# Rotations of k and q in PSUM, and low parts of plain weights in two operations

## The chip, the cores and the metric

The kernel runs on one core of one Trainium2 chip. The metric is the device time of one execution in microseconds (us), the median of several runs. TensorE (PE) multiplies, VectorE (DVE), ScalarE (ACT) and GpSimd (POOL) do the elementwise work, SyncE (SP) issues the transfers. SBUF is the on-chip memory, PSUM the eight banks that TensorE writes its products to.

## The reference

A two-layer streaming encoder step, in fp32: 1024 frames of a new stream (the prompt) and 64 frames of a running one (the sample), 1088 columns of 1024 features. Layer 0 is a gated short convolution. Layer 1 is latent attention with rotated parts of q and k, and this is where most of the change lies:

```
def apply_rope(x, cos, sin):
    x1, x2 = xf[..., :QK_ROPE_DIM // 2], xf[..., QK_ROPE_DIM // 2:]
    out = jnp.concatenate([x1 * cos - x2 * sin, x2 * cos + x1 * sin], axis=-1)

def mla_project(h, pos, w_in, q_norm_g, w_qb, kv_norm_g):
    p = h @ w_in                       # q_lat 256, kv_lat 128, k_rope 32, z 1024
    q = (rms_norm(q_lat, q_norm_g) @ w_qb).reshape(B, T, N_HEADS, QK_DIM)
    q_rope = apply_rope(q[..., QK_NOPE_DIM:], cos[:, None, :], sin[:, None, :])
    k_rope = apply_rope(k_rope, cos, sin)
    c_kv = rms_norm(kv_lat, kv_norm_g)
    return q, c_kv, k_rope, z
```

After it come attention (16 heads, a mask by chunks of 64 frames for the prompt, 512 cached keys for the sample), `silu(z) * o` times an output matrix, a residual add and a last norm.

## The kernel before

**Accuracy.** Every fp32 product is three products of a reduced type: each operand is split into a high part (a copy by ScalarE into that type, `hi`) and a low part (`raw - hi`), and hi·hi, hi·lo and lo·hi are added up in PSUM. So each weight of 128x1024 costs a transfer (L287), a copy by ScalarE (L288) and a subtraction. `load_w` (L274) gives the subtraction to GpSimd (L292) unless it is told otherwise. The conv weights that are used in combinations are split by other lines (L636, L637), which stay as they are.

**Stages.** Columns are taken in three chunks of 384, 384 and 320 (`CHK`), features in eight tiles of 128. Layer 0 fills the time to about 510 us. Then comes the front of layer 1 (to about 590 us), sample attention (to 675), prompt attention, and from about 985 us the output projection.

**The front of layer 1.** Nine tiles of latents are made with `latent_mm` and leave PSUM by `latent_evac` (VectorE, L1059). The q latents are normed into `QNH`, `QNL` (high and low) with `QNS` for the sample (L1011). Then the loop at L1141 makes k's 32 rotated rows for each chunk c: 16 products with `wrs`, ScalarE copies half the result to SBUF (`t1`, L1155), and VectorE adds the other half (L1156), multiplies by the norm `r1` (L1157), swaps the halves of the 32 rows (`stream_shuffle`, L1158), multiplies by sin (L1159) and cos (L1160) and adds (L1161). In the trace `t1` and `t2` are called kt. In between, the generator `c_norm` norms the kv latents: it makes `csh` and `csl` (L351, L352) of each chunk, which TensorE sums over the partitions with a matrix of ones, and `sample_q` makes the sample's q from `QNS`.

Then `q_rope(g, c)` (L1204) rotates q for four groups of heads, g, and three chunks, c, twelve times: six products into a bank of PSUM, shuffle (L1212), times sin on GpSimd (L1213), times cos on VectorE (L1216), sum (L1217), high part by ScalarE (L1219), low part on VectorE (L1222), and two transfers out (L1224). `t1` and `t2` are called qt in the trace, `qlo` is qrl.

**What sets the order.** Between these steps stand half tiles of the gate projection (`z_stream`, L1014: 24 products for each chunk, then one multiplication on VectorE out of PSUM, L1031, and the next weight after a tile's first chunk). How many half tiles follow each step is written in tables (`ZA`, `ZC`, `ZR`, L973). Within that, a scheduler at build time orders each engine's queue. All matmuls of these stages are recorded at one line, L301. PSUM is one tile PS of eight banks; `split_psum` divides it into rings, here z of banks 0 and 1 and g of banks 2 to 7, and `gps` takes the next bank of a ring in turn, so a product waits until the last reader of that bank is done.

Of the kernel before, what the change touches and what calls it, by code (L numbers as in the profile page):

```python
# [11 lines left out]
F32 = mybir.dt.float32  # L12
# [29 lines left out]
def r32(ap):  # L42
    return ap.bitcast(F32)
# [166 lines left out]
def kernel(ctx, tc, xT, small, w1, w2, w3, w3r, wpair, wqr, wv, wkT, w4,  # L210
# [3 lines left out]
    V, A, G, PE, SP = nc.vector, nc.scalar, nc.gpsimd, nc.tensor, nc.sync  # L214
# [9 lines left out]
    def nm(s):  # L224
        cnt[0] += 1
        return f"{s}_{cnt[0]}"

    PS = ctx.enter_context(tc.tile_pool(name="ps", bufs=1, space=PSUM)).tile([P, 8, 512], F32, name="PS")
    turns = {}

    def split_psum(**first):

        turns.clear()
        turns.update({k: [v, 0] for k, v in first.items()})

    def gps(tag="g", size=1):
        (b0, b1), k = turns[tag]
        turns[tag][1] = (k + size) % (b1 - b0)
        return PS[:, b0 + k:b0 + k + size, :].rearrange("p b n -> p (b n)")
# [27 lines left out]
    def ordered(ins):  # L267
        if keep_order[0]:
            tc.keep_in_program_order(ins)

    WN = [1024, 2]
    hi_on, lo_on = [None], [None]

    def load_w(src, n, view=None, into=None, lo_engine=None, cuts=None, shared=False):  # L274
        raw = wp[0].tile([P, WN[0]], F32, tag="wraw", name=nm("wraw"), bufs=3)
        if into is None:
            hi = wp[0].tile([P, WN[0]], F32R, tag="whi", name=nm("whi"), bufs=WN[1])
            lo = wp[0].tile([P, WN[0]], F32R, tag="wlo", name=nm("wlo"), bufs=WN[1])
        else:
            hi, lo = into  # L280
        if cuts:
            def part(a, b):
                ordered(A.copy(out=hi[:, a:b], in_=raw[:, a:b]))
                ordered((lo_engine or G).tensor_sub(lo[:, a:b], raw[:, a:b], r32(hi[:, a:b])))
            return hi, lo, lambda a, b: SP.dma_start(out=raw[:, a:b], in_=src[:, a:b]), part
        dst = raw[:, :n] if view is None else view(raw[:, :n])
        SP.dma_start(out=dst, in_=src)  # L287
        ins = A.copy(out=hi[:, :n], in_=raw[:, :n])  # L288
        hi_on[0] = ins.ins
        ordered(ins)  # L290
        m = n // 2 if shared else n
        ins = (lo_engine or G).tensor_sub(lo[:, :m], raw[:, :m], r32(hi[:, :m]))  # L292
        lo_on[0] = ins.ins
        ordered(ins)
        if shared:
            V.tensor_sub(lo[:, m:n], raw[:, m:n], r32(hi[:, m:n]))
        return hi, lo
# [86 lines left out]
    def xh(k, c0, c1):  # L384
        return XHV[:, k, c0:c1]
# [153 lines left out]
    def new_u(ct, sc):  # L539
        u = p1.tile([P, SC + 4], F32, tag="u", name=nm("u"), bufs=1)  # L540
        if sc == 0:
            V.memset(u[:, 0:2], 0.0)
        return u

    def new_z():
        return p1.tile([P, SC], F32, tag="z", name=nm("z"), bufs=1)
# [251 lines left out]
    for ct in range(STD):  # L798
        if ct == 0:
            u, z = new_u(ct, 0), new_z()  # L800
# [68 lines left out]
        else:  # L869
            for pi, part in enumerate(PARTS):  # L870
# [4 lines left out]
                for c in range(2):  # L875
                    ps = conv_mm(c, W, (KD, 0)[c])
                    if ct == 1 and pi == c == 0:
                        rest()
                    if pi == c == 0:
                        u, z = new_u(ct, 0), new_z()  # L880
# [55 lines left out]
    for dt in range(KD):  # L936
        wh, wl = load_w(w2[dt], 1024)
        g = sm[:, C_NG + 8 + dt:C_NG + 9 + dt]
# [3 lines left out]
        for c, (c0, c1) in enumerate(CHK):  # L942
            n = c1 - c0
            x = xr[c]
            ps = gps()
# [23 lines left out]
    p1.release()  # L969


    split_psum(z=(0, 2), g=(2, 8))
    ZA, ZC, ZR, ZQ, ZB, ZS = (0, 1), 1, (0, 2, 1, 1), (0, 1, 1, 1, 3, 0, 1, 0), (1, 2, 3), ((1, 2, 2, 1), (1, 2, 2, 1), (1, 2, 2, 1), (1, 2, 1, 0))  # L973
    SIL, ZG = ((0,), (1,), (2,), (3, 4), (5, 6)), (1, 1, 1, 0)
    pz = tc.alloc_tile_pool(name="pz", bufs=1, reuse_waits="tile")
# [17 lines left out]
    p3t = tc.alloc_tile_pool(name="p3t", bufs=1, reuse_waits="tile")  # L993

    cosb, sinb = SZ[:, 6, :], SZ[:, 7, :]
    ql = [SZ[:, 2, :], SZ[:, 3, :], SZ[:, 4, :]]
    kr = SZ[0:ROPE, 5, :]
# [3 lines left out]
    SHUF = [(i + 16) % 32 for i in range(32)]  # L1001
    r1 = acc1
# [5 lines left out]
    def split(hi, lo, src, lo_engine=None):  # L1008
        ins = A.copy(out=hi, in_=src)
        ordered(ins)  # L1010
        ordered((lo_engine or V).tensor_sub(lo, src, r32(hi)))  # L1011
        return ins.ins
# [82 lines left out]
    ps = latent_mm(2, 0)  # L1095
    q_rstd(1, sq1)
    latent_evac(2, 0, ps)
    ps = latent_mm(2, 1)
# [48 lines left out]
    for c, (c0, c1) in enumerate(CHK):  # L1147
        n = c1 - c0
        ps = gps("z")
        for k in range(KD):  # L1150
            mm(ps[:2 * ROPE, :n], wrs3[:, k, :], xh(k, c0, c1), k == 0, False)
            mm(ps[:2 * ROPE, :n], wrs3[:, k, :], xl(k, c0, c1), False, k == KD - 1)
        t1 = p3t.tile([P, 512], F32, tag="qt1", name=nm("kt1"), bufs=2)[:ROPE]
        t2 = p3t.tile([P, 512], F32, tag="qt2", name=nm("kt2"), bufs=2)[:ROPE]
        A.copy(out=t1[:, :n], in_=ps[ROPE:2 * ROPE, :n])  # L1155
        V.tensor_add(t1[:, :n], ps[:ROPE, :n], t1[:, :n])  # L1156
        V.tensor_mul(t1[:, :n], t1[:, :n], r1[:ROPE, c0:c1])  # L1157
        V.stream_shuffle(t2[:, :n], t1[:, :n], SHUF)  # L1158
        V.tensor_mul(t2[:, :n], t2[:, :n], sinb[:ROPE, c0:c1])  # L1159
        V.tensor_mul(t1[:, :n], t1[:, :n], cosb[:ROPE, c0:c1])  # L1160
        V.tensor_add(kr[:, c0:c1], t1[:, :n], t2[:, :n])  # L1161
        if c == 0:
            for f in range(2):
                split(QNH[:, f, :], QNL[:, f, :], ql[f], G if f else None)
    next(cns)
    SP.dma_start(out=o_kr, in_=kr)
    split(KR[0:32, :], KR[32:64, :], kr[:, :SEQ])

    def add_halves(out, ps3):

# [33 lines left out]
    def q_rope(g, c):  # L1204
        c0, c1 = CHK[c]
        n = c1 - c0
        wh, wl = (x[:, g * 256:(g + 1) * 256] for x in WR)
        ps = gps()
        gemm(ps[:, :n], lambda k: wh[:, k * P:(k + 1) * P], lambda k: wl[:, k * P:(k + 1) * P],
             lambda k: QNH[:, k, c0:c1], lambda k: QNL[:, k, c0:c1], 2)  # L1210
        t2 = p3t.tile([P, 512], F32, tag="qt2", name=nm("qt2"), bufs=2)
        ordered(V.stream_shuffle(t2[:, :n], ps[:, :n], SHUF))  # L1212
        G.tensor_mul(t2[:, :n], t2[:, :n], sinb[:, c0:c1])  # L1213
        yield
        t1 = p3t.tile([P, 512], F32, tag="qt1", name=nm("qt1"), bufs=2)
        ordered(V.tensor_mul(t1[:, :n], ps[:, :n], cosb[:, c0:c1]))  # L1216
        ordered(V.tensor_add(t1[:, :n], t1[:, :n], t2[:, :n]))  # L1217
        qh = p3t.tile([P, 512], F32R, tag="qrh", name=nm("qrh"), bufs=2)
        ordered(A.copy(out=qh[:, :n], in_=t1[:, :n]))  # L1219
        yield  # L1220
        qlo = p3t.tile([P, 512], F32R, tag="qrl", name=nm("qrl"), bufs=2)
        ordered(V.tensor_sub(qlo[:, :n], t1[:, :n], r32(qh[:, :n])))  # L1222
        for s, t in ((0, qh), (1, qlo)):
            SP.dma_start(out=qr_d[s, 4 * g:4 * g + 4, :, c0:c1].rearrange("h r t -> (h r) t"), in_=r32(t[:, :n]))  # L1224

# [39 lines left out]
    for g in range(4):  # L1265
# [3 lines left out]
        if g == 2:  # L1269
            ps = gps()  # L1270
# [142 lines left out]
    pk = tc.alloc_tile_pool(name="pk", bufs=1, reuse_waits="tile")  # L1413
# [285 lines left out]
    for n in ends:  # L1699
        if isinstance(n, int):  # L1700
            split_gated(448, 832, [n])
        else:
            name = n[0], H - 1, n[1]
# [122 lines left out]
    for dt in range(KD):  # L1826
# [136 lines left out]
```

## Time and profile before

| | |
|---|---|
| median of 3 runs | 1089.97 us (1088.22 to 1091.15) |
| the profiled execution | 1086.63 us, its span 1084.8 us, 1.83 us around it |
| mean granted clock of TensorE | 0.989 of full speed |
| PE busy | 1045.5 us (96%), 7123 matmuls |
| PE weight loads busy | 1002.3 us (92%) |
| DVE busy | 746.9 us (69%) |
| ACT busy | 638.2 us (59%) |
| POOL busy | 528.4 us (49%) |

Busy shares are means over stages that differ. A row of the timeline gives the start in us from the beginning of the span, the duration, the engine, the line, the operation, output <- inputs, shapes, how many, and in brackets the idle time ahead of it with what ended it. A row of the windows gives the stretch, its length, the busy us (and number of instructions) of PE, its weight loads, DVE, ACT and POOL, then TensorE's granted clock as a share of full speed, the DMA engines' busy share and GB/s.

### The profile page before, as it was taken

To read this page: it belongs to the slowest core of one execution; us is meant where nothing else is said; L and a number is where in the kernel's file an instruction comes from. 1 tells how busy PE (TensorE), PEld (TensorE's weight loads), DVE (VectorE), ACT (ScalarE), POOL (GpSimd) and SP (SyncE) were. 2 spreads that over 40 slices of the span, in tenths; PEclk is the share of its full clock that TensorE was granted. 3 is DMA by queue.
4 is the path that set the end of the run, shared out by engine and by line. 5 is a ranking of instruction groups with operands and counts; after the bars stand their busy time and mean duration, and the time that the engine had idled before them with its cause. 6 is when DMAs were issued, how large, how long until landed. Compare 5 with 4: busy or idle time off the path is not lost.

```text
span 1084.8 us, 19669 instructions
## 1 busy us (share of the span) xinstructions
PE 1045.5 (96%) x7123; PEld 1002.3 (92%) x7123; DVE 746.9 (69%) x1523; ACT 638.2 (59%) x1388; POOL 528.4 (49%) x446
## 2 busy tenths in 40 slices
PE   9979999999999999999898999999999999999997
PEld 8979999989999999999798999899999999898996
DVE  6787666756666545564997442688888888888346
ACT  6456676666666634344532434777877787786434
POOL 0476598896666622212443322354645555465225
PEclk9999999999999999999898999999999999999999
DMA  7244233333223244432232113544233412326225
GB/s 239 70 128 134 106 110 109 128 130 118 98 98 114 78 141 142 131 104 72 82 126 100 50 34 92 120 93 106 57 71 89 105 50 60 79 67 213 95 83 204
DMA packets 58145, 114.55 MB, mean 106 GB/s; under 512 B 8080, under 2 KB 32400, under 8 KB 58048
## 3 DMA queue, kind: packets, MB, share of 16 engines
q1 hardware_dynamic: 57840, 112.97, 34.3%
q8 instruction: 56, 0.92, 0.4%
q14 instruction: 41, 0.34, 0.1%
q10 hardware_dynamic: 144, 0.26, 0.1%
q0 software_dynamic: 64, 0.07, 0.0%
HBM read 79.27 MB, written 16.31 MB: 88 GB/s over the span
## 4 chain that ended last, share of the span: by engine, by line
PE 74%; DVE 11%; ACT 4%; POOL 3%; DMA 3%; issue 3%; SPq 1%; POOLq 0%; DVEq 0%; ACTq 0%
PE PS L301 52%; PE PS L1487 17%; PE PS L1526 5%; DMA QB<-stg 2%; DVE PS L488 1%; POOL wlo L292 1%; DVE OL L1011 1%; ACT PH L1539 1%; ACT stg L1603 1%; POOL R L565 1%; POOL R L513 0%; DMA wraw<-in_w 0%; DVE qt L1212 0%; DVE SZ L367 0%; SPq L1613 0%
## 5 line engine op out<-in xcount | busy, mean ns | idle before, releaser
L301 PE MATMUL PS<-R,whi 128*128 128x272 f32 (+2 forms) x1662 | 370.3, 312 | 14.8 <-ACT whi L288 4.4
L301 PEld LDWEIGHTS PS<-R,whi 128*128 128x128 f32 x1662 | 276.9, 191 | 18.9 <-ACT whi L288 5.1
L301 PE MATMUL PS<-R,wlo 128*128 128x272 f32 (+2 forms) x888 | 266.8, 312 | 2.3 <-POOL wlo L292 2.3
L292 POOL TENSOR_TENSOR wlo<-wraw,whi 128x1024 fp32r<-128x1024 f32 x36 | 88.6, 2462 | 185.5 <-ACT whi L288 172.8
L301 PEld LDWEIGHTS PS<-R,wlo 128*128 128x128 f32 x888 | 165.0, 191 | 3.4 <-POOL wlo L292 3.0
L1487 PE MATMUL PS<-KB,QB 96*128 96x512 f32 (+11 forms) x576 | 125.1, 354 | 1.1 <-DVE SZ L1031 0.6
L1521 POOL TENSOR_SCALAR Pt<-Pt,st 128x640 f32<-128x640 f32 (+3 forms) x64 | 61.4, 961 | 86.2 <-DVE st L1517 85.6
L1487 PEld LDWEIGHTS PS<-KB,QB 96*128 96x128 f32 (+1 forms) x576 | 94.3, 190 | 9.5 <-DVE PL L1543 1.1
L1504 DVE TENSOR_REDUCE st<-PS 128x1 f32<-128x1024 f32 (+7 forms) x128 | 94.7, 748 | 10.9 <-PE PS L1487 10.2
L1543 DVE TENSOR_TENSOR PL<-PS,PH 128x512 fp32r<-128x512 f32 (+3 forms) x192 | 98.7, 547 | 3.1 <-ACT PH L1539 1.8
L1539 ACT CAST PH<-PS 128x512 fp32r<-128x512 f32 (+3 forms) x192 | 85.3, 496 | 14.7 <-PE PS L1526 13.4
L1487 PE MATMUL PS<-PH,VB 128*128 128x256 f32 x320 | 76.5, 279 | 0.0
L637 POOL TENSOR_TENSOR wlo<-wraw,whi 128x1024 fp32r<-128x1024 f32 x26 | 62.5, 2404 | 26.8 <-ACT whi L636 26.5
L1487 PE MATMUL PS<-PL,VB 128*128 128x256 f32 x320 | 75.2, 281 | 0.2 <-DVE PL L1543 0.2
L1513 ACT ACTIVATE Pt<-PS,st 128x640 f32<-128x640 f32 (+3 forms) x64 | 62.1, 970 | 5.7 <-DVE st L1517 2.6
L301 PE MATMUL PS<-R,bhi 128*128 128x272 f32 x320 | 61.1, 289 | 2.3 <-DVE z L763 1.0
L1487 PEld LDWEIGHTS PS<-PH,VB 128*128 128x128 f32 x320 | 60.7, 190 | 1.3 <-DVE PL L1543 0.8
L1487 PEld LDWEIGHTS PS<-PL,VB 128*128 128x128 f32 x320 | 61.0, 191 | 0.7 <-DVE PL L1543 0.4
L288 ACT CAST whi<-wraw 128x1024 fp32r<-128x1024 f32 (+1 forms) x37 | 38.2, 1034 | 39.1 <-PE PS L301 20.6
L1526 PE MATMUL PS<-ident,Pt 128*128 128x128 f32 x416 | 55.4, 274 | 0.2 <-ACT Pt L1513 0.2
L1568 POOL TENSOR_TENSOR SZ<-SZ,ot 64x256 f32<-64x256 f32 x64 | 47.0, 744 | 11.6 <-DVE ot L1563 9.4
L301 PEld LDWEIGHTS PS<-R,bhi 128*128 128x128 f32 x320 | 49.6, 188 | 3.3 <-DVE z L763 1.2
(435 smaller groups left out, 2607.1 us busy)
## 6 DMA issues: line engine op xcount, KB each, us to landing
wraw<-in_w SPq DMA_DIRECT2D x83, 512.0 KB, 3.6
KB<-stg SPq DMA_DIRECT2D x32, 256.0 KB, 3.8
QB<-stg SPq DMA_DIRECT2D x32, 256.0 KB, 4.6
braw<-in_w SPq DMA_DIRECT2D x13, 512.0 KB, 4.4
QB<-qr_scratch SPq DMA_DIRECT2D x32, 128.0 KB, 3.0
x<-x_scratch SPq DMA_DIRECT2D x8, 416.0 KB, 3.2
xr<-in_xT SPq DMA_DIRECT2D x16, 192.0 KB, 2.5
x_scratch<-xr SPq DMA_DIRECT2D x16, 192.0 KB, 1.8
```

The costliest lines, as they stand in the source:

```text
L288: ins = A.copy(out=hi[:, :n], in_=raw[:, :n])
L292: ins = (lo_engine or G).tensor_sub(lo[:, :m], raw[:, :m], r32(hi[:, :m]))
L301: ins = PE.matmul(ps, lhsT, rhs, start=start, stop=stop, skip_group_check=more)
L637: ins = eng.tensor_sub(lo, src, r32(hi))
L1487: pin(PE.matmul(ps, lhsT, rhs, start=start, stop=stop))
L1504: pin(V.tensor_reduce(out=st[:, 0:1], in_=TL["S", h, i], axis=AX.XY, op=ALU.max, negate=True))
L1513: pin(A.activation(out=Pt, in_=TL.pop(("S", h, i)), func=AF.Exp, bias=st[:, 0:1], accum_out=st[:, 1:2]))
L1521: pin(G.tensor_scalar(Pt, Pt, st[:, 2:3], 1.0, op0=ALU.mult, op1=ALU.mult))
L1526: pin(PE.transpose(out=tp[:, j * P:(j + 1) * P], in_=TL["P", h, i][:, (j0 + j) * P:(j0 + j + 1) * P], identity=ident))
L1539: pin(A.copy(out=hi, in_=src))
L1543: pin(V.tensor_sub(lo, src, r32(hi)))
L1568: pin(G.tensor_mul(sz, sz, TL.pop(("ot", h, pr))[rows]))
```

## The change

Three edits.

1. `load_w`: where GpSimd forms the low part of a weight of 1024 columns, it does so in two subtractions of 512 columns.
2. PSUM is divided into z of banks 0 to 3 and g of banks 4 to 7 through the latents and the rotation of k; after that into z of 0 and 1 and g of 2 to 7 as before, the next bank of g being bank 4.
3. The rotations work in place in PSUM. For k: the sum, the product with `r1`, the shuffle, the product with cos and the last sum read PSUM, and the product with sin moves from VectorE to GpSimd. For q: product with cos, sum, high part and low part read PSUM, and the bank is held until the low part is made (L1222, before: L1216).

```
+        c = m // 2 if lo_engine is None and m == 1024 else m
+        for a in range(0, m, c):
+            ins = (lo_engine or G).tensor_sub(lo[:, a:a + c], raw[:, a:a + c], r32(hi[:, a:a + c]))
...
-    split_psum(z=(0, 2), g=(2, 8))
+    split_psum(z=(0, 4), g=(4, 8))
...
-        V.tensor_add(t1[:, :n], ps[:ROPE, :n], t1[:, :n])
-        V.tensor_mul(t1[:, :n], t1[:, :n], r1[:ROPE, c0:c1])
-        V.stream_shuffle(t2[:, :n], t1[:, :n], SHUF)
-        V.tensor_mul(t2[:, :n], t2[:, :n], sinb[:ROPE, c0:c1])
-        V.tensor_mul(t1[:, :n], t1[:, :n], cosb[:ROPE, c0:c1])
-        V.tensor_add(kr[:, c0:c1], t1[:, :n], t2[:, :n])
+        pk = ps[:ROPE, :n]
+        V.tensor_add(pk, pk, t1[:, :n])
+        V.tensor_mul(pk, pk, r1[:ROPE, c0:c1])
+        V.stream_shuffle(t2[:, :n], pk, SHUF)
+        G.tensor_mul(t2[:, :n], t2[:, :n], sinb[:ROPE, c0:c1])
+        V.tensor_mul(pk, pk, cosb[:ROPE, c0:c1])
+        V.tensor_add(kr[:, c0:c1], pk, t2[:, :n])
...
+    split_psum(z=(0, 2), g=(2, 8))
+    turns["g"][1] = 2
...
-        t1 = p3t.tile([P, 512], F32, tag="qt1", name=nm("qt1"), bufs=2)
-        ordered(V.tensor_mul(t1[:, :n], ps[:, :n], cosb[:, c0:c1]))
-        ordered(V.tensor_add(t1[:, :n], t1[:, :n], t2[:, :n]))
+        t1 = ps[:, :n]
+        ordered(V.tensor_mul(t1, t1, cosb[:, c0:c1]))
+        ordered(V.tensor_add(t1, t1, t2[:, :n]))
...
-        ordered(A.copy(out=qh[:, :n], in_=t1[:, :n]))
+        ordered(A.copy(out=qh[:, :n], in_=t1))
...
-        ordered(V.tensor_sub(qlo[:, :n], t1[:, :n], r32(qh[:, :n])))
+        ordered(V.tensor_sub(qlo[:, :n], t1, r32(qh[:, :n])))
```

Three places in which the queues differ. Lines of the changed kernel lie a few further down: L1156 to L1158 are L1159 to L1161, L1160 and L1161 are L1163 and L1164, L292 is L294, L352 is L354, and the product with sin is L1162.

First VectorE, in the rotation of k, from the second chunk's first sum (kt_612 and kt_613 before, kt_612 and kt_613_6000 after) to `csl`. Before:

```order
L1156 TENSOR_TENSOR kt_612_5977<-PS,kt_612_5977 32x384
L1161 TENSOR_TENSOR SZ<-kt_610_5948,kt_611_5949 32x384
L1157 TENSOR_TENSOR kt_612_5977<-kt_612_5977,acc_100 32x384
L1158 STREAM_SHUFFLE kt_613_5978<-kt_612_5977 32x384
L1156 TENSOR_TENSOR kt_614_6002<-PS,kt_614_6002 32x320
L1159 TENSOR_TENSOR kt_613_5978<-kt_613_5978,SZ 32x384
L1160 TENSOR_TENSOR kt_612_5977<-kt_612_5977,SZ 32x384
L1157 TENSOR_TENSOR kt_614_6002<-kt_614_6002,acc_100 32x320
L1161 TENSOR_TENSOR SZ<-kt_612_5977,kt_613_5978 32x384
L1158 STREAM_SHUFFLE kt_615_6003<-kt_614_6002 32x320
L352 SCALAR_TENSOR_TENSOR csl_6049<-SZ,eps_88,csh_6048 128x384
```

And after:

```order
L1159 TENSOR_TENSOR PS<-PS,kt_612_5999 32x384
L1164 TENSOR_TENSOR SZ<-PS,kt_611_5971 32x384
L1160 TENSOR_TENSOR PS<-PS,acc_100 32x384
L1161 STREAM_SHUFFLE kt_613_6000<-PS 32x384
L1163 TENSOR_TENSOR PS<-PS,SZ 32x384
L1159 TENSOR_TENSOR PS<-PS,kt_614_6024 32x320
L1164 TENSOR_TENSOR SZ<-PS,kt_613_6000 32x384
L1160 TENSOR_TENSOR PS<-PS,acc_100 32x320
L354 SCALAR_TENSOR_TENSOR csl_6071<-SZ,eps_88,csh_6070 128x384
```

The product with sin is gone from this queue, every other operation has PS in place of one SBUF input, `csl` moves ahead of the third chunk's shuffle, and the last sum of a chunk (SZ<-PS) stands behind the next chunk's first sum, as before.

Second GpSimd at the same place. Before:

```order
L292 TENSOR_TENSOR CKL<-wraw_5925,CKH 128x1024
L292 TENSOR_TENSOR wlo_5915<-wraw_5913,whi_5914 128x1024
L1011 TENSOR_TENSOR QNL<-SZ,QNH 128x1088
L1192 TENSOR_TENSOR wk_6260<-wraw_6258,wk_6259 128x256
L292 TENSOR_TENSOR wlo_6113<-wraw_6111,whi_6112 128x1024
```

And after:

```order
L294 TENSOR_TENSOR CKL<-wraw_5946,CKH 128x512 x2
L294 TENSOR_TENSOR wlo_5935<-wraw_5933,whi_5934 128x512 x2
L1013 TENSOR_TENSOR QNL<-SZ,QNH 128x1088
L1198 TENSOR_TENSOR wk_6279<-wraw_6277,wk_6278 128x256
L1162 TENSOR_TENSOR kt_611_5971<-kt_611_5971,SZ 32x384
L1162 TENSOR_TENSOR kt_613_6000<-kt_613_6000,SZ 32x384
L1162 TENSOR_TENSOR kt_615_6025<-kt_615_6025,SZ 32x320
L294 TENSOR_TENSOR wlo_6135<-wraw_6133,whi_6134 128x512 x2
```

The three products with sin stand behind `QNL` and the sample's weight wk, and ahead of the next weight's low part, which is now two rows.

Third TensorE near the end of the twelve rotations of q: the end of one gate half tile (weight whi, wlo, inputs R and XLB) and what follows it. Before, the sample's absorbed q (QS, wk) follows:

```order
L301 MATMUL PS<-R_98,whi_6339 128x384
L301 MATMUL PS<-XLB,whi_6339 128x384
L301 MATMUL PS<-R_98,wlo_6340 128x384
L301 MATMUL PS<-QS,wk_6259 128x128
L301 MATMUL PS<-QS,wk_6260 128x128
```

And after:

```order
L303 MATMUL PS<-R_98,whi_6356 128x384
L303 MATMUL PS<-XLB,whi_6356 128x384
L303 MATMUL PS<-R_98,wlo_6357 128x384
L303 MATMUL PS<-R_98,whi_6356 128x320 x2
L303 MATMUL PS<-R_98,wlo_6357 128x320
L303 MATMUL PS<-R_98,whi_6356 128x320 x2
L303 MATMUL PS<-R_98,wlo_6357 128x320
L303 MATMUL PS<-R_98,whi_6356 128x320 x2
L303 MATMUL PS<-R_98,whi_6356 128x384 x2
L303 MATMUL PS<-R_98,wlo_6357 128x384
```

Eight products of the third chunk (128x320), which go to the same bank of z as the first chunk's tile that ends just above them, now come directly behind it; then the second chunk follows, and the absorbed q comes behind that.

## Rows read from the trace of the kernel before

**Rows 1.** Windows of three stretches (columns: see the profile above).

```profile
520.00:540.00 20.00, 15.98 (x91) 13.64 (x90) 18.88 (x33) 7.52 (x15) 8.82 (x4) 0.87 0.22 66
560.00:590.00 30.00, 26.13 (x143) 25.38 (x142) 27.55 (x47) 7.59 (x13) 13.53 (x10) 0.89 0.36 120
590.00:675.00 85.00, 84.92 (x559) 81.74 (x558) 31.68 (x66) 33.34 (x75) 23.45 (x26) 1.00 0.20 59
```

**Rows 2.** Timeline of TensorE, 523 to 577 us.

```profile
523.28 0.92 PE L301 MATMUL PS<-R,wrs 128*64 128x384 f32 x4 [2.12 <-DVE SZ L1059]
...
530.02 0.22 PE L301 MATMUL PS<-QNS,whi 128*128 128x128 f32 x1
...
538.27 0.67 PE L301 MATMUL PS<-csl,ones 128*128 128x384 f32 x1 [1.91 <-DVE csl L352]
...
576.95 0.98 PE L301 MATMUL PS<-R,whi 128*128 128x384 f32 x2 [3.81 <-DVE SZ L1031]
```

**Rows 3.** Windows behind each of those three waits, columns as in rows 1.

```profile
523.28:528.50 5.22, 5.22 (x22) 3.84 (x23) 4.26 (x7) 4.08 (x8) 2.31 (x1) 0.67 0.35 104
538.27:542.20 3.93, 3.93 (x14) 3.93 (x14) 3.90 (x8) 2.65 (x5) 1.28 (x1) 0.57 0.16 35
576.95:583.00 6.05, 6.05 (x20) 6.05 (x21) 5.44 (x14) 0.90 (x3) 2.02 (x2) 0.53 0.36 131
```

**Rows 4.** Timeline of VectorE, 526 to 538 us.

```profile
526.21 0.22 DVE L1011 TENSOR_TENSOR QNS<-SZ,QNS 128x64 fp32r<-128x64 f32 x1
526.64 0.55 DVE L1156 TENSOR_TENSOR kt<-PS,kt 32x384 f32<-32x384 f32 x1 [0.21 <-ACT kt L1155]
527.22 1.99 DVE L1157 TENSOR_TENSOR kt<-kt,acc 32x384 f32<-32x384 f32 x1
529.25 0.57 DVE L1158 STREAM_SHUFFLE kt<-kt 32x384 f32<-32x384 f32 x1
...
531.74 0.54 DVE L1157 TENSOR_TENSOR kt<-kt,acc 32x384 f32<-32x384 f32 x1
...
533.66 2.75 DVE L1160 TENSOR_TENSOR kt<-kt,SZ 32x384 f32<-32x384 f32 x1
...
537.62 0.59 DVE L352 SCALAR_TENSOR_TENSOR csl<-SZ,eps,csh 128x384 fp32r<-128x384 f32 x1
```

**Rows 5.** Timeline of GpSimd, 526 to 536 us.

```profile
526.19 2.61 POOL L1011 TENSOR_TENSOR QNL<-SZ,QNH 128x1088 fp32r<-128x1088 f32 x1 [3.71 <-ACT QNH L1009]
528.76 1.05 POOL L1192 TENSOR_TENSOR wk<-wraw,wk 128x256 fp32r<-128x256 f32 x1
533.29 2.71 POOL L292 TENSOR_TENSOR wlo<-wraw,whi 128x1024 fp32r<-128x1024 f32 x1 [3.48 <-ACT whi L288]
```

**Rows 6.** Groups by line, VectorE's part of q's rotations: busy us, mean ns.

```profile
L1217 DVE TENSOR_TENSOR qt<-qt,qt 128x384 f32<-128x384 f32 (+1 forms) x12 | 11.8, 984 | 0.9
...
L1222 DVE TENSOR_TENSOR qrl<-qt,qrh 128x384 fp32r<-128x384 f32 (+1 forms) x12 | 10.1, 840 | 0.2 <-ACT qrh L1219 0.2
...
L1216 DVE TENSOR_TENSOR qt<-PS,SZ 128x384 f32<-128x384 f32 (+1 forms) x12 | 6.2, 517 | 0.0
```

**Rows 7.** Timeline of VectorE, 573 to 577 us.

```profile
573.64 2.69 DVE L1222 TENSOR_TENSOR qrl<-qt,qrh 128x384 fp32r<-128x384 f32 x1
576.26 0.94 DVE L1031 TENSOR_TENSOR SZ<-PS,acc 128x384 f32<-128x384 f32 x2
```

**Rows 8.** Timeline of GpSimd, 564 to 576 us.

```profile
564.48 1.01 POOL L1213 TENSOR_TENSOR qt<-qt,SZ 128x384 f32<-128x384 f32 x1 [1.29 <-DVE qt L1212]
...
573.27 2.65 POOL L292 TENSOR_TENSOR wlo<-wraw,whi 128x1024 fp32r<-128x1024 f32 x1
```

**Rows 9.** Windows, GpSimd's L292 alone: us, POOL busy, clock, transfers.

```profile
0.00:110.00 110.00, 20.00 (x8) 0.98 0.45 144
```

**Rows 10.** Timeline of GpSimd in layer 0.

```profile
61.88 2.47 POOL L534 TENSOR_TENSOR z<-z,acc 128x272 f32<-128x272 f32 x1 [2.23 <-ACT z L533]
```

**Rows 11.** Waits of TensorE: us in total, times, longest us.

```profile
PE PS L301 <- POOL wlo L292: 2.3, 3, 1.6
```

More of the change, by code (lines that the diff above doesn't have):

```diff
@@ L291, in load_w @@
         m = n // 2 if shared else n
-        ins = (lo_engine or G).tensor_sub(lo[:, :m], raw[:, :m], r32(hi[:, :m]))
-        lo_on[0] = ins.ins
-        ordered(ins)
+        c = m // 2 if lo_engine is None and m == 1024 else m
+        for a in range(0, m, c):
+            ins = (lo_engine or G).tensor_sub(lo[:, a:a + c], raw[:, a:a + c], r32(hi[:, a:a + c]))
+            lo_on[0] = ins.ins
+            ordered(ins)
         if shared:
```

## Prediction, made before the changed kernel ran

> **What bounds the kernel now.** I read the windows first, to find where TensorE isn't busy, then its timeline there for what ended each wait, and then VectorE's and GpSimd's timelines for why the releaser was late. Two windows matter [rows 1]. From 520 to 540 us VectorE is busy 18.88 of 20 us and TensorE 15.98; from 560 to 590 us VectorE 27.55 of 30 and TensorE 26.13. The reader is to see that VectorE is the full engine there and TensorE waits for it. From 590 to 675 us TensorE is busy 84.92 of 85 us at full clock, so a start that comes earlier is carried on to the end.
>
> TensorE waits three times in the front of layer 1 [rows 2]: 2.12 us at 523.28 for the multiplication that empties a latent tile's bank (the ring z has two), 1.91 us at 538.27 for csl, 3.81 us at 576.95 for the multiplication L1031. That is 7.84 us. [...] What this costs against full clock is 5.22 x 0.33 + 3.93 x 0.43 + 6.05 x 0.47 = 1.7 + 1.7 + 2.8 = 6.3 us. Waits and clock are 14.1 us together: all that these stretches can give.
>
> Why VectorE is late: L1157 took 1.99 us the first time and 0.54 the second [rows 4], and in the first case GpSimd ran QNL from 526.19 to 528.80 [rows 5]. L1160 took 2.75 us, started at 533.66, and GpSimd ran a low part of a weight from 533.29 to 536.00 [rows 4, 5]. L1222 took 2.69 us from 573.64, beside a low part from 573.27 to 575.92 [rows 7, 8]. Each had two inputs in SBUF and ended some 0.4 us behind GpSimd's operation: they were held until it ended. L1156, with one input in PSUM, began at 526.64 under that same QNL and took 0.55 [rows 4]. So does the group L1216 (one input in PSUM): a mean of 517 ns over twelve, where L1217 and L1222, of the same size with both inputs in SBUF, have 984 and 840 [rows 6]. The change gives just these operations an input in PSUM.
>
> **The change, part by part.**
>
> *VectorE in q's rotations* (L1217 and L1222): 12 x (984 - 517) = 5.6 us and 12 x (840 - 517) = 3.9 us less. TensorE needs only what it waits for: the 3.81 us at 576.95 and the clock behind it, 2.8, 6.7 us. L1031 came at 576.26 only because L1222 of 2.69 stood ahead of it [rows 7]; at 0.52 it would come 2.2 us sooner, and three or four of the earlier L1217 and L1222 at the mean saving, 0.3 to 0.5 each, give the other 1.6. I take the wait as gone: **6.7 us**. Lower bound: 2.2 us of it, with the clock still falling.
>
> *VectorE in k's rotation.* With four banks for z, the first chunk's products no longer wait for the bank: 2.12 and 1.7 us go, and TensorE begins with QNS at 526.2 instead of 530.02 [rows 2]. It needs 6.3 us from there to the wait for csl (538.27 - 1.91 - 530.02), and is there at 532.5. VectorE's chain to csl still starts at 526.64, since ScalarE's copy and QNS [rows 4] are where they were: L1156, L1157 (no longer held) and the shuffle, 0.55 + 0.54 + 0.57, to about 528.3. Then the product with sin waits for GpSimd, which does QNL to 528.80 and wk (1.05) to 529.8 [rows 5], and takes 1.01 us for it by L1213 [rows 8], to about 530.8. From there the chain is the first chunk's last sum, the second's L1157 and shuffle, GpSimd's second product, the second's last sum, the third's L1157 and csl: 0.5 + 0.5 + 0.6 + 1.0 + 0.5 + 0.5 + 0.6 = 4.2, to 535.0, where csl ended at 538.2 [rows 4]. TensorE arrives at 532.5 and still waits some 2.5 us, so the clock still falls. The stretch ends 3.2 us earlier; I take **3.1 us** on, since the third chunk's csl has a GpSimd product ahead of it and the next low part beside it. Bounds: nothing, if the products on GpSimd cost what the banks give; 7.4 us (3.8 for the first wait and 3.6 for the second with its clock) if both waits go.
>
> *GpSimd.* Three products with sin come to it (1.0 us each), in a stretch where it is busy 8.82 of 20 us [rows 1]; what they add to the path is counted above.
>
> *TensorE's order at the end of q's rotations.* Eight products of the gate's third chunk now stand right behind the first chunk's tile in the same bank, so they wait for L1031 of that tile: 0.94 us for two [rows 7], about 0.5 for one and 0.2 to start it: **-0.7 us**. If VectorE is behind there, up to one held operation more.
>
> *Split low parts.* Of 37 weights eight fall in the first 110 us, 2.50 us each [rows 9]. By L1213's 1.01 us for 384 columns [rows 8], 512 take 1.35, so two halves 2.7: 0.2 more, which GpSimd's idle time covers in nearly all of the span. Gain at most the 2.3 us that TensorE waits for low parts at all [rows 11], if the first half releases it earlier; loss in the rivals. I take **0**, since TensorE's waits for low parts are three in the whole span.
>
> Sum: 6.7 + 3.1 - 0.7 + 0 = 9.1 us. The profiled execution, 1086.63 us (span 1084.8 and 1.83 around it), becomes 1077.5. It lies 3.3 us below the median of the runs, so I put the same gain on the median: 1089.97 - 9.1 = 1080.9 us.
>
> [...] At equal size, L1156 out of PSUM and the unhindered L1157 out of SBUF take 0.55 and 0.54 us [rows 4]: a PSUM input costs nothing here. [...]
>
> **The rivals.**
>
> *All three waits go with their clocks.* For it: TensorE's wait for csl is only 2.5 us long in my chain, and a scheduler may put csl early. Against: csl stands behind two GpSimd products in the queue. Gain 14.1 us, 1075.9; with the sin products a little late, 12 to 15.5.
>
> *The rotation of k slips.* QNL on GpSimd started at 526.19 and QNS on VectorE at 526.21, both with inputs in SBUF [rows 4, 5]: whichever is first holds the other. VectorE won, barely. If GpSimd is first, QNS and all k operations behind it come 2.4 us later (528.80 against 526.4), and L1156's early start is lost. Then k's part gives 3.1 - 2.4 = 0.7 and the total is 6.7; with one more held operation of the size of L1160's 2.75, 4.0. Between them about 1084.7.
>
> *The change doesn't do what it says.* q's bank is now held until L1222, not L1216. If TensorE then waits for g's banks, or for the absorbed q behind them, the wait of 3.81 us moves instead of going, and only k's part is left: gain 0 to 3.3. For it: VectorE is 92% busy there [rows 1]. Against: six banks, and three operations of 0.5 us more each.
>
> *Slower: second halves pushed behind VectorE.* Between two halves GpSimd gives up SBUF, and a VectorE operation with two SBUF inputs can get in front of the second half. How that looks is shown at 61.88: a GpSimd product of 272 columns took 2.47 us [rows 10], where L1213's rate gives 0.7: 1.8 held. Layer 0's start has eight split weights [rows 9], and TensorE waits for low parts there [rows 11]. 8 x 1.8 = 14.4 us; it exceeds the gain of 9.1 from the sixth weight on (5.1 x 1.8). With all eight, 1089.97 - 9.1 + 14.4 = 1095.3. Against: one such row in that stretch, and a half that comes late matters only where TensorE has caught up with it, three times so far. [...]
>
> **How the numbers follow.** A measurement of this kernel tells about 0.3%, 3.3 us, from no change. Chances: the forecast (gain 7 to 12) 0.52; all waits gone 0.15; k slips (4 to 7) 0.15; the wait moves (0 to 3.3) 0.10; second halves pushed 0.08, of which 0.07 ends over 3.3 us slower. Faster 0.52 + 0.15 + 0.15 = 0.82, same 0.11, slower 0.07. The time is the forecast's, 1080.9. The range takes the forecast, nearly all of the first rival (gain 15) and the second down to a gain of 3.5: 1075.0 to 1086.5, with 0.18 left out.
>
> **What would show it.** In the profile after: L1157's successor without a row near 2 us, L1222's mean near 0.52 to 0.6; no wait near 523 with clock 0.67; csl some 3.2 us sooner with a wait of about 2.5 us ahead of it; the 3.81 us wait gone and VectorE at about 0.8 of 560 to 590 us; a wait of under 1 us for L1031 near its end. In layer 0 nothing but more GpSimd instructions. I am wrong if a wait over 2 us for L1222 or L1031 stands in that stretch, if QNS starts behind QNL, or if TensorE's waits for low parts pass 2.3 us in the first 110.

## The result and the profile after

The changed kernel takes 1077.08 us (median of 4 runs, 1075.36 to 1080.87) against 1089.1 for the kernel before (median of 4): ratio 0.9894, 95% interval 0.9866 to 0.9922, that is 8.5 to 14.6 us faster. The forecast was 1080.9 in a range of 1075.0 to 1086.5. The profiled execution is the slowest of the four: 1080.87 us, span 1079.1.

The windows that answer to [rows 1], then the front of layer 1 as a whole, first of the kernel after:

```profile
520.00:540.00 20.00, 16.48 (x109) 14.75 (x108) 17.44 (x31) 10.62 (x19) 12.67 (x10) 1.00 0.26 75
560.00:590.00 30.00, 29.97 (x189) 29.17 (x188) 20.60 (x49) 9.87 (x22) 13.30 (x13) 1.00 0.36 124
515.00:600.00 85.00, 81.25 (x516) 77.77 (x516) 66.23 (x139) 36.77 (x77) 42.77 (x37) 1.00 0.31 106
```

and the same 85 us of the kernel before:

```profile
515.00:600.00 85.00, 77.03 (x447) 72.87 (x446) 74.53 (x131) 32.84 (x66) 35.36 (x26) 0.92 0.30 100
```

From 560 to 590 us TensorE is full now, 29.97 of 30 us, and VectorE fell from 27.55 to 20.60. Over the 85 us TensorE works 4.2 us more and at full clock instead of 0.92: 0.08 x 85 = 6.8 us. Of these 6.8 us some 0.5 fell in the wait of 3.81 us, where TensorE had nothing to do. The gain has two parts, then, waits of 4.2 and clock of 6.3, 10.5 us together, and the second is the larger one.

TensorE's waits in this stretch after, to set against [rows 2]:

```profile
534.36 0.44 PE L303 MATMUL PS<-csl,ones 128*128 128x384 f32 x1 [1.64 <-DVE csl L354]
538.92 0.41 PE L303 MATMUL PS<-csl,ones 128*128 128x320 f32 x1 [1.89 <-DVE csl L354]
546.34 0.56 PE L303 MATMUL PS<-R,whi 128*128 128x320 f32 x2 [0.20 <-DVE SZ L1033]
```

The wait for a latent's bank (2.12) and the wait of 3.81 are gone. That for csl is a little shorter and has a second one behind it, for the third chunk.

VectorE's groups in the rotation of q, to set against [rows 6]:

```profile
L1223 DVE TENSOR_TENSOR PS<-PS,qt 128x384 f32<-128x384 f32 (+1 forms) x12 | 6.5, 541 | 1.9 <-POOL qt L1219 1.1
L1222 DVE TENSOR_TENSOR PS<-PS,SZ 128x384 f32<-128x384 f32 (+1 forms) x12 | 6.5, 540 | 0.0
L1228 DVE TENSOR_TENSOR qrl<-PS,qrh 128x384 fp32r<-128x384 f32 (+1 forms) x12 | 6.3, 526 | 0.1
```

The sum fell from a mean of 984 ns to 541, the low part from 840 to 526; the product with cos, which now also writes to PSUM, rose from 517 to 540. VectorE in the rotation of k, rows chosen from 526 to 539 us (against [rows 4]):

```profile
526.91 0.55 DVE L1160 TENSOR_TENSOR PS<-PS,acc 32x384 f32<-32x384 f32 x1
...
530.07 0.55 DVE L1164 TENSOR_TENSOR SZ<-PS,kt 32x384 f32<-32x384 f32 x1 [1.06 <-POOL kt L1162]
...
533.71 0.60 DVE L354 SCALAR_TENSOR_TENSOR csl<-SZ,eps,csh 128x384 fp32r<-128x384 f32 x1
...
536.63 1.65 DVE L1254 COPY SZ<-SZ 32x64 f32<-32x64 f32 x1
538.32 0.55 DVE L354 SCALAR_TENSOR_TENSOR csl<-SZ,eps,csh 128x320 fp32r<-128x320 f32 x1
```

and GpSimd beside it (against [rows 5]):

```profile
525.87 2.51 POOL L1013 TENSOR_TENSOR QNL<-SZ,QNH 128x1088 fp32r<-128x1088 f32 x1 [1.71 <-DVE QNL L1013]
528.35 0.73 POOL L1198 TENSOR_TENSOR wk<-wraw,wk 128x256 fp32r<-128x256 f32 x1
529.04 1.00 POOL L1162 TENSOR_TENSOR kt<-kt,SZ 32x384 f32<-32x384 f32 x1
```

The product with the norm (L1160 now) runs beside QNL in 0.55 us, where it was held for 1.99. VectorE then waits 1.06 us for GpSimd's product with sin, which stands behind QNL and wk, and csl ends at 534.31 in place of 538.21.

### The profile page after: what moved, and what is told of

Same layout as the page of the kernel before. It is cut to its first block, busy times and chain, and to the rows that moved or that the text cites. A ratio compares the mean times of both kernels' runs of the same rounds, so it can differ in the third digit from the quotient of the medians.

```text
span 1079.1 us, 19733 instructions
## 1 busy us (share of the span) xinstructions
PE 1045.8 (97%) x7123; PEld 1003.0 (93%) x7123; DVE 723.3 (67%) x1520; ACT 638.0 (59%) x1388; POOL 540.3 (50%) x486
## 4 chain that ended last, share of the span: by engine, by line
PE 79%; DVE 8%; ACT 4%; DMA 4%; POOL 3%; issue 2%; SPq 1%; POOLq 0%; ACTq 0%; DVEq 0%
PE PS L303 55%; PE PS L1493 18%; PE PS L1532 5%; DMA QB<-stg 2%; DMA wraw<-in_w 1%; POOL wlo L294 1%; DVE OL L1013 1%; DVE PS L490 1%; POOL R L567 1%; ACT PH L1545 1%; ACT stg L1609 0%; DVE ST L572 0%; DVE PL L1549 0%; DMA wraw<-in_wpair 0%; DVE SZ L1088 0%
## 5 line engine op out<-in xcount | busy, mean ns | idle before, releaser
L303 PE MATMUL PS<-R,whi 128*128 128x272 f32 (+2 forms) x1662 | 369.3, 312 | 10.5 <-ACT whi L288 4.0
L294 POOL TENSOR_TENSOR wlo<-wraw,whi 128x512 fp32r<-128x512 f32 x72 | 99.3, 1399 | 174.6 <-ACT whi L288 159.5
L1493 PE MATMUL PS<-KB,QB 96*128 96x512 f32 (+11 forms) x576 | 128.0, 361 | 1.3 <-DMA QB<-stg 0.7
L1493 PEld LDWEIGHTS PS<-KB,QB 96*128 96x128 f32 (+1 forms) x576 | 96.5, 194 | 10.1 <-DVE PL L1549 1.1
L1510 DVE TENSOR_REDUCE st<-PS 128x1 f32<-128x1024 f32 (+7 forms) x128 | 94.7, 747 | 13.5 <-PE PS L1493 12.8
L639 POOL TENSOR_TENSOR wlo<-wraw,whi 128x1024 fp32r<-128x1024 f32 x26 | 62.4, 2401 | 26.2 <-ACT whi L638 25.9
L1527 POOL TENSOR_SCALAR Ph<-Ph,st 128x512 f32<-128x512 f32 (+3 forms) x64 | 34.0, 532 | 40.1 <-DVE st L1523 30.7
```

The lines of the kernel that those rows point to most:

```text
L294: ins = (lo_engine or G).tensor_sub(lo[:, a:a + c], raw[:, a:a + c], r32(hi[:, a:a + c]))
L303: ins = PE.matmul(ps, lhsT, rhs, start=start, stop=stop, skip_group_check=more)
L639: ins = eng.tensor_sub(lo, src, r32(hi))
L1493: pin(PE.matmul(ps, lhsT, rhs, start=start, stop=stop))
L1510: pin(V.tensor_reduce(out=st[:, 0:1], in_=TL["S", h, i], axis=AX.XY, op=ALU.max, negate=True))
L1527: pin(G.tensor_scalar(Pt, Pt, st[:, 2:3], 1.0, op0=ALU.mult, op1=ALU.mult))
```

## The experiments

All twelve are timed against the kernel before on the same chip; a gain in us is the ratio's, on 1088. The table sums what their profiles show from 515 to 600 us, one execution each: TensorE's idle time, and the time lost to the clock, which is each window of 2.5 us times one minus its granted clock, added up. A low clock while TensorE idles is in both of these columns and counts once in the last. The table leaves out e7_csl, which computes other values.

| kernel | ratio to before (95%) | idle, us | clock, us | together |
|---|---|---|---|---|
| before | 1 | 8.0 | 6.9 | 14.2 |
| changed, first and second profile | 0.9894 (0.9866 to 0.9922), 0.9894 (0.9869 to 0.9919) | 3.8, 3.7 | 0, 0 | 3.8, 3.7 |
| e1_split | 0.9976 (0.9963 to 0.9989) | 9.3 | 0 | 9.3 |
| e2_banks | 0.9995 (0.9981 to 1.0009) | 9.0 | 5.1 | 13.2 |
| e3_k | 0.9973 (0.9959 to 0.9987) | 8.7 | 1.7 | 10.4 |
| e4_q | 0.9934 (0.9915 to 0.9952) | 4.1 | 1.7 | 5.8 |
| e5_rot | 0.9904 (0.9889 to 0.9919) | 3.3 | 1.7 | 4.8 |
| e6_sin_v | 0.9902 (0.9888 to 0.9916) | 3.4 | 3.4 | 6.3 |
| e8_split8 | 1.0002 (0.9990 to 1.0014) | 9.3 | 5.1 | 13.3 |
| e9_csl | 0.9927 (0.9902 to 0.9952) | 5.6 | 1.7 | 7.3 |
| e10_csl_whole | 0.9929 (0.9905 to 0.9953) | 1.5 | 5.1 | 6.6 |
| e12_lo_v | 0.9977 (0.9963 to 0.9990) | 7.4 | 3.4 | 10.8 |

### The split alone

```
 load_w: two subtractions of 512 columns; all else as before
```

> Only the two subtractions of 512 columns; rotations and banks as before. Theory: in the first 110 us TensorE's waits for low parts (1.62 and 0.44 us in the timeline of before, 2.3 us in the table of waits) go, since the first four products of a tile need only the first half: 2.0 to 2.5 us faster there; in the rotations of q a held VectorE operation waits for a half, so the 3.81 us wait becomes 2.4 to 3.8: 0 to 1.4 more. Together 2 to 4 us faster. Rival (the shorter layer 0 of the changed kernel's profile is chance): within 1 us of before, with the waits for low parts still there. Rival (second halves pushed behind VectorE): GpSimd's halves wait in pairs and the kernel is slower by 1 us or more.

1085.75 us, 2.6 us faster (1.2 to 4.0). In layer 0 TensorE's waits for low parts fell to one of 0.20 us. But in the profile the front of layer 1 lost no clock although TensorE idled longer there (9.3 us against 8.0). A held operation now waits for one half and the next for the other (GpSimd is busy 2.50 of 2.50 us from 535 to 537.5, with two instructions); VectorE's timeline of this kernel has the pair in place of L1160's 2.75 us [rows 4]:

```profile
535.25 1.63 DVE L1162 TENSOR_TENSOR kt<-kt,SZ 32x384 f32<-32x384 f32 x1
536.82 1.56 DVE L1159 TENSOR_TENSOR kt<-kt,acc 32x320 f32<-32x320 f32 x1
```

So the split doesn't shorten the hold here, it divides it: 1.63 + 1.56 us for two operations that took 2.75 and 0.47 before. Earlier in the front it does shorten one. The first chunk's csl, with two SBUF inputs, is held beside CKL's low part on GpSimd (517.40 to 519.84 in the kernel before); first before, then this kernel in a second fence:

```profile
517.96 2.30 DVE L352 SCALAR_TENSOR_TENSOR csl<-SZ,eps,csh 128x384 fp32r<-128x384 f32 x1
```

```profile
520.83 1.18 DVE L354 SCALAR_TENSOR_TENSOR csl<-SZ,eps,csh 128x384 fp32r<-128x384 f32 x1
```

From the start of this csl to the end of the second QNS VectorE needs 7.2 us in the four profiles with all low parts split (e1_split, e6_sin_v, the changed kernel's two), and 8.5 to 8.7 us in the seven with CKL's whole; e9_csl and e10_csl_whole, which form csl in another order, are not among them. So the split brings VectorE to the rotation of k 1.3 us sooner. Where the 2.6 us come from was left to a run of its own:

```
+        c = m // 2 if lo_engine is None and m == 1024 and n_lo[0] < 8 else m
+        n_lo[0] += m == 1024 and lo_engine is None
```

> Before with two subtractions for the first eight low parts only, those of the first 110 us. Theory (the whole gain of the split is there, where TensorE waits for low parts): 2 to 3.2 us faster than before, as with all of them split (2.1 median, ratio 0.9976), the waits for low parts under 0.4 us, the front of layer 1 as before. Rival (it comes from shorter holds in the front of layer 1): within 0.7 us of before.

Ratio 1.0002: nothing, so my theory for the split fell. The waits for low parts are gone in this profile, but they differ from one profile to the next: 0.7 to 2.3 us in the seven with whole low parts in the first 110 us, 0 to 1.6 in the six with split ones (0 and 0.7 for the changed kernel, 1.6 for e6_sin_v). What is lost in their place here stands in the windows of 60 to 110 us, first before, then e8_split8 in a second fence:

```profile
60.00:110.00 50.00, 41.80 (x322) 40.25 (x321) 40.04 (x90) 29.21 (x57) 31.69 (x17) 1.00 0.46 148
```

```profile
60.00:110.00 50.00, 43.98 (x316) 42.52 (x315) 38.00 (x85) 28.60 (x55) 31.04 (x21) 0.93 0.44 139
```

TensorE is busy 2.2 us more, at a clock of 0.93, which costs 3.5 us; before loses 1.7 us to the clock earlier, from 7.5 to 15 us, where e8_split8 loses none. Over the whole 110 us TensorE's idle time falls from 11.5 to 9.8 us, and the time lost to the clock rises from 1.7 to 3.4. Over the thirteen profiles of the table the first 110 us lose 3.4 us to the clock in five of the six with split low parts there (none in e6_sin_v), and 1.7 in six of the seven with whole ones (5.1 in e12_lo_v). Idle time and clock together come to 11.4 to 13.5 us with split and 11.1 to 13.9 with whole low parts, so the split gains nothing in layer 0 that can be told. By elimination the 2.6 us of e1_split lie behind the first 110 us, but where is not shown: its profile has 4.9 us less in the front of layer 1, in clock and not in waits, and yet its span is only 0.4 us shorter than that of before (1084.4 and 1084.8).

### The banks alone, the banks with k, and q alone

```
 e2_banks: split_psum(z=(0, 4), g=(4, 8)) through k's rotation; all else as before
 e3_k:     the same, and k's rotation in PSUM with its product with sin on GpSimd
 e4_q:     q's rotation in PSUM; banks, k and low parts as before
```

> Only the four z banks up to the end of k's rotation; nothing reads PSUM that did not before, low parts whole. Theory (VectorE's chain to csl is the bound, banks only let TensorE run ahead): the 2.12 us wait at k's first products goes and the wait for csl grows by about as much, to 3.5 to 5.7 us; csl ends within 0.7 us of 538.2; gain 0 to 1.7 us (the clock behind the first wait). Rival (TensorE waited for banks, VectorE's holds are off the path): 3 to 4 us faster, csl's wait stays near 1.9.

Ratio 0.9995, no difference, as the theory had it. The wait for the bank is gone, and csl's is what it was plus the time that TensorE came earlier:

```profile
538.90 0.69 PE L301 MATMUL PS<-csl,ones 128*128 128x384 f32 x1 [5.48 <-DVE csl L352]
```

1.91 became 5.48, csl ended at 538.84: VectorE's chain is the bound, and banks by themselves give nothing.

> Four z banks and the rotation of k in PSUM with its product with sin on GpSimd; q's rotation and low parts as before. Theory: as in the changed kernel up to 545 us: the 2.12 wait goes, csl ends near 534.3, the wait for it stays between 1.6 and 2.6; the 3.81 us wait in q's rotations stays (3 to 4.5 us). 3 to 5.5 us faster (3.8 with the clock after csl low, 5.5 with it full). Rival (k's part gives nothing by itself because the rotations of q are the next bound): within 1 us of before, the later wait grows to 6 us or more.

2.9 us faster (1.4 to 4.5), just under the 3 to 5.5 expected. TensorE waits 2.03 and 1.74 us for csl, and the wait for L1031 in q's rotations is 4.1 us, as expected. Csl ends at 535.52, 1.2 us later than expected: I had taken 534.3 from the changed kernel, where the split brings VectorE to k's rotation 1.3 us sooner.

> Only q's rotation in PSUM; banks, k's rotation and low parts as before. Theory (an operation with two SBUF inputs is held while GpSimd runs, one with a PSUM input is not): L1217's and L1222's successors fall from means of 984 and 840 ns to 520 to 560, the 3.81 us wait goes with the low clock behind it: 5 to 7 us faster. Rival (the bank is held until the low part is made and TensorE waits for banks instead): 0 to 2.5 us faster, with a wait of 1 us or more for the low part in that stretch.

7.2 us faster (5.2 to 9.3). The groups read as in the changed kernel (means of 542 and 526 ns), the window of 560 to 590 us has TensorE busy 30.00 of 30 us, and no wait for a bank came in place of the 3.81. The three parts by themselves sum to 2.6 + 2.9 + 7.2 = 12.7 us; the change as a whole measured 11.5, and with intervals this wide the two agree.

### The change without the split, and with sin on VectorE

> The whole change without the two operations: low parts in one subtraction of 1024 columns. Theory (the split acts in layer 0 alone; the rotations no longer have two SBUF inputs that a low part could hold): before minus 9 to 10.5 us, that is 2 to 3 us slower than the changed kernel, with TensorE's waits for low parts back at 1 to 2.3 us and the front of layer 1 as in the changed kernel. Rival (the split also shortens holds on the rotations' path): front of layer 1 longer by 1 us or more as well, 4 us slower than the changed kernel. Rival (split is chance): as the changed kernel, minus 11 to 13.

1078.42 us, 10.4 us faster (8.8 to 12.1), and TensorE waits 1.1 us for low parts: both within the theory's ranges. But the ratio, 0.9904, is only 1.1 us from the changed kernel's 0.9894 and not the 2 to 3 expected: the split is worth nothing that can be told once the rotations read PSUM. The front of layer 1 has 4.8 us in the table against the changed kernel's 3.8 and 3.7, in line with the 1.3 us by which VectorE comes later to k's rotation without the split; this much of the first rival is there.

> The whole change, but k's product with sin stays on VectorE, with both inputs in SBUF. Theory (what matters is the number of held operations ahead of csl): the first such product meets QNL on GpSimd and is held until it ends, about 0.6 to 1.2 us, the second is free or meets the next low part and is held by 1.3 to 1.6 us; but the waits for GpSimd's own products (1.06, 0.26 and 0.65 us of VectorE idle in the changed kernel) go. csl ends within 1.2 us of the changed kernel's 534.3; time within 1.5 us of the changed kernel. Rival (the move to GpSimd is what shortened the chain): csl ends 2 us or more later and the kernel is 2 to 4 us slower than the changed one.

1077.76 us. Csl ends at 534.07 and the third chunk's at 534.86, so TensorE waits once, 3.37 us, in place of twice. One product with sin was held (1.02 us), two were not (0.53 and 0.47). That this product moved to GpSimd is worth nothing that can be told, either way; my theory held.

### Is it GpSimd that holds them?

The rotations stay in SBUF, and GpSimd's low parts are taken away from beside them:

```
-                    W[f + 1] = load_w(w3[4 + f], 1024)
+                    W[f + 1] = load_w(w3[4 + f], 1024, lo_engine=V)
```

> Before, with the rotations out of SBUF as they were, but the low parts of seven of the gate's weights (L292) on VectorE instead of GpSimd, so that GpSimd has only its product with sin beside the rotations of q and nothing beside the second chunk of k. Theory (an operation with two SBUF inputs is long only because GpSimd runs beside it): the second chunk's L1160 falls from 2.75 us to 0.54, no L1222 is longer than 1.4 us (the product with sin, 1.01, is still there) where one took 2.69, means of L1217 and L1222 700 ns or less; VectorE gets three or four low parts of 1.2 us in this stretch in exchange. Csl's wait goes (it was 1.91), the 3.81 us wait shrinks to under 2; 1 to 6 us faster than before. Rival (two SBUF inputs are slow in that stretch by themselves, whatever GpSimd does): L1160 and L1222 still show rows over 2 us without a low part beside them, time within 1 us of before or slower by the low parts, up to 4 us.

VectorE's timeline of this kernel, k's rotation:

```profile
528.01 1.99 DVE L1157 TENSOR_TENSOR kt<-kt,acc 32x384 f32<-32x384 f32 x1
...
534.45 0.54 DVE L1160 TENSOR_TENSOR kt<-kt,SZ 32x384 f32<-32x384 f32 x1
```

and its groups, with the low parts that VectorE took over (seven of the eight):

```profile
L292 DVE TENSOR_TENSOR wlo<-wraw,whi 128x1024 fp32r<-128x1024 f32 (+1 forms) x8 | 9.8, 1222 | 5.7 <-ACT whi L288 5.7
L1217 DVE TENSOR_TENSOR qt<-qt,qt 128x384 f32<-128x384 f32 (+1 forms) x12 | 9.6, 801 | 0.7
L1222 DVE TENSOR_TENSOR qrl<-qt,qrh 128x384 fp32r<-128x384 f32 (+1 forms) x12 | 7.1, 593 | 0.3 <-DMA qr_scratch<-qrl 0.3
```

The same instruction L1160, with the same two SBUF inputs, takes 0.54 us in place of 2.75 when no low part runs beside it, while L1157, which still meets QNL, takes 1.99 as before. L1222's mean falls from 840 to 593; L1217's stays at 801, above the 700 that I expected of both, since GpSimd's product with sin is still there (1.04 us from 564.59, beside the product from 564.20 to 565.21, and 0.54 from 578.12, beside none). That is the cause of the holds, shown. Csl's wait is gone. The gain is only 2.5 us (1.1 to 4.0): VectorE pays 1.2 us for each low part and is late elsewhere, so that the longest wait in q's rotations is 3.32 us, where I expected under 2:

```profile
568.94 0.56 PE L301 MATMUL PS<-R,whi 128*128 128x320 f32 x2 [3.32 <-DVE SZ L1031]
```

That L1031 stands behind one of the low parts (567.19, 1.23 us).

### Taking away the waits that are left

The changed kernel waits 3.5 us for csl. Three kernels form these parts sooner:

```
+            if c == 1:
+                hi, lo = KR[:, :n], KR[:, 512:512 + n]
...
+        if c == 2:
+            next(cns)
```

with the first call ahead of k's loop. In e7_csl the split of the rotated k, which writes KR, still stood ahead of the sum over KR, so the second chunk's norm was formed from other values.

> The whole change, and the kv latents' high and low parts for the second and third chunk are formed sooner: the second's in KR, which is free until then, before k's rotation, the third's in the buffer that k's weights leave, ahead of the third chunk's rotation. Theory (after the change TensorE waits only for csl, 1.64 and 1.89 us, because it stands behind the rotation of k on VectorE): both waits go or fall under 0.5 us, 2 to 3.5 us faster than the changed kernel. Rival (another VectorE operation behind the same chain is late next, the sample's sums or the norm): the waits move to a product behind the sample's sums, gain under 1 us.

It took 1082.21 us (ratio 0.9941, 0.9929 to 0.9954), and TensorE waited 7.34 us for that write to KR: it says nothing on the theory. With the write behind the sums:

> As the run before it with csl formed sooner, with the split of the rotated k behind the last sum of the kv latents, so that KR still holds the second chunk's parts when they are summed. Theory (in the changed kernel TensorE waits 1.64 and 1.89 us only because csl stands behind k's rotation): both waits under 0.5 us, 2 to 3.5 us faster than the changed kernel, 13 to 15.5 us faster than before. Rival (the next operation behind the same chain on VectorE is late instead): the waits move to a product behind the sample's sums or the norm, under 1 us faster than the changed kernel.

> The same without the two operations, low parts whole. Theory (splitting the first eight low parts took TensorE's waits for them away and gave nothing in time, so the split is worth nothing once the rotations read PSUM): within 1.5 us of the run with them. Rival (the split is worth the 2.6 us that it gave by itself): 2 to 3.5 us slower than the run with them.

> The changed kernel once more, unaltered, on the same chip as the two others: a ratio of 0.987 to 0.992 to before as at first; it is the base for both, and its profile shows whether the two waits for csl (1.64 and 1.89 us) and the clock of the first 110 us (0.93 from 60 to 110 us) are the same in another execution.

1080.33 us with the split, 1080.84 without, 1077.16 for the changed kernel beside them. Both waits for csl are gone, as the theory had it, and both kernels are some 3 us slower than the changed one: the slowest of its six executions, 1077.92 us, is faster than any of theirs. The theory of the gain fell, and what the rival names came instead, at another product: VectorE is late behind the same chain. In e9_csl another operation with two SBUF inputs, the low part of the sample's q, took 3.59 us, with GpSimd busy through 537.5 to 540 us (2.50 of 2.50), where it took 0.41 in e6_sin_v with GpSimd idle, and VectorE's queue is late behind it; first VectorE, then TensorE's longest wait in the stretch, in a second fence of the same kernel:

```profile
536.77 3.59 DVE L1013 TENSOR_TENSOR QS<-qst,QS 128x256 fp32r<-128x256 f32 x1
```

```profile
547.77 0.57 PE L303 MATMUL PS<-R,whi 128*128 128x320 f32 x2 [3.74 <-DVE SZ L1033]
```

In e10_csl_whole TensorE waits only 1.27 and 0.21 us in the whole stretch, and the clock falls:

```profile
530.00:540.00 10.00, 10.00 (x41) 10.00 (x41) 8.21 (x16) 2.84 (x6) 6.24 (x6) 0.55 0.00 0
```

Busy all the time at 0.55: 4.5 us lost in ten. The two are less different than they look. In e10_csl_whole the low part of the sample's q is held as well (3.42 us from 537.31, GpSimd again busy 2.50 of 2.50 from 537.5 to 540), and VectorE's multiplication that TensorE waits for in the second fence (it ends at 547.71) ends at 548.10 in e10_csl_whole. TensorE at its low clock needs its products just as late, and so waits only the 0.21 us. By the table e9_csl and e10_csl_whole have 3.6 and 2.9 us more in this stretch than the changed kernel, and their medians are 3.2 and 3.7 us higher. That the two are within 1.5 us of one another was expected and held. No version measured faster than the changed kernel.

## Why the prediction was right, and where its sum was off

**The bound.** Right: VectorE sets the pace of both windows, banks alone give nothing (e2_banks, ratio 0.9995), and the holds come from GpSimd's operations beside two SBUF inputs (e12_lo_v, 0.54 us in place of 2.75 without one).

**q's rotations, 6.7 us.** Right: 7.2 measured for that part alone, with the wait and its clock gone. VectorE's share of 560 to 590 us fell further than to the 0.8 forecast, to 0.69.

**k's rotation, 3.1 us.** Right in size, 2.9 alone. The chain came out as added up, with VectorE idle for GpSimd's product as forecast: from the end of the second QNS to the end of csl it took 8.3 us in e3_k and in the changed kernel, forecast 8.6 (526.4 to 535.0), before 11.8. That csl ended at 534.31 in the changed kernel, sooner still, comes from the 1.3 us by which the split brings VectorE there sooner. The wait was 1.64 us, forecast 2.5. Two things were not seen. The third chunk's csl brought a wait of 1.89 us, for which I had taken off 0.1: VectorE's copy L1254 was held for 1.65 us by the low part that I had named (535.73 to 538.24), right ahead of it. And I left the clock low behind csl (1.7 us), where both profiles of the changed kernel have full clock from 515 to 600 us. The two nearly cancel, which is luck.

**TensorE's new order, -0.7 us.** Wrong. The eight products began while the multiplication that was to free their bank had not:

```profile
575.34 0.45 PE L303 MATMUL PS<-R,whi 128*128 128x320 f32 x2
```

```profile
575.54 0.56 DVE L1033 TENSOR_TENSOR SZ<-PS,acc 128x384 f32<-128x384 f32 x1 [0.28 <-PE PS L303]
```

They wait for nothing, so they go to another bank: I had read the ring wrong, in the section on the change too. The first chunk's tile is the seventh to take a bank of z behind the rotation of k, so it has bank 0; then `split_psum(z=(0, 2), ...)` at L1286 of the changed kernel starts the ring over at bank 0. It is the second chunk that shares the bank and has to wait, and the third goes to bank 1. TensorE works on the eight products while VectorE frees bank 0, and has no idle time there.

**Split low parts, 0 us.** Right in sum, for other reasons than the one given. In layer 0 five of the six profiles with split low parts lose more to the clock, and idle time and clock together are no lower with them. In the front of layer 1 the split shortens VectorE's way to k's rotation by 1.3 us, which the prediction did not see; in time nothing of it can be told (e5_rot). The rival of the second halves being pushed showed no loss in time (ratios 1.0002 and 0.9976), though a push is there: CKL's two halves took 3.18 us from 517.97 in the changed kernel, beside csl and VectorE's L369, and the pair from 26.56 took 2.53.

**The sum.** The 6.3 us that the prediction puts on the clock are each window of [rows 3], its length times one minus its clock, added up. Forecast 9.1, measured 11.5 (8.5 to 14.6): the difference is within the interval. By the profiles the front of layer 1 gave 10.5 us, 1.4 more than forecast, and 1.3 of these can be named: 0.9 for the shorter wait for csl, 1.7 for the clock behind it and 0.7 for TensorE's order, less 1.8 for the third chunk's wait and 0.2 for one at 546 us. That the profiled execution gained only 5.7 us in its span has a place: it lost 3.4 us to the clock at 677 to 688 us, where the profile of before and the changed kernel's second profile (span 1073.5) lost none, and 3.4 us more than before ahead of 515 us. The profiles of e4_q and e5_rot lose 3.4 and 5.1 us from 677 to 690 us as well; whether the change brings this about in some executions was not tried.

**The near tie** of QNL and QNS fell as before: QNS at 525.77, QNL at 525.87.

**What a PSUM input costs.** The prediction had it from two rows that it costs nothing. Unheld, the low part takes 0.54 to 0.56 us out of SBUF (e12_lo_v) and 0.55 out of PSUM (changed), 384 columns in both: that held. The product with cos, which had its PSUM input before, rose by 23 ns (mean of 517 to 540) when its output went to PSUM as well.

## What to carry to other kernels

Where VectorE bounds a stretch and GpSimd works beside it, look for rows of VectorE with two SBUF inputs that end just behind a GpSimd row: giving such an operation one input in PSUM took it from 840 and 984 ns to some 530 without moving any work. A copy with its one input in SBUF can be held too (L1254, 1.65 us beside GpSimd and 0.18 in e6_sin_v, where GpSimd was idle). Banks that only let TensorE arrive earlier gave nothing here (0.9995) while VectorE's chain set the end. Dividing GpSimd's operation in two shortened one hold (2.30 to 1.18 us) and only passed half of another on to the next operation. Count TensorE's granted clock beside its waits, and time a version that takes waits away before believing it: here 3.5 us of waits removed cost 3 us in the end.

## What was not expected

TensorE's clock doesn't follow the length of the waits. Before, the clock fell behind waits of 2.12 and 1.91 us and during one of 3.81 (6.9 us lost); in e1_split waits that sum to more (9.3 us idle) lost nothing, in the changed kernel 1.64 and 1.89 lost nothing, and in e10_csl_whole a wait of 1.27 us was followed by 5.1 us lost. In layer 0 a stretch with shorter waits (43.98 us busy of 50 against 41.80) ran at 0.93 in place of 1.00. e1_split and e8_split8 idle the same 9.3 us in the front of layer 1 and lose 0 and 5.1 us to the clock. Which pattern of work brings the clock down was not tried and stays open.
